# Indexer keys gathered once and transposed on TensorE, indexer queries projected before the keys

## The chip, the core and the metric

The kernel runs on one core of one Trainium2 chip. The metric is the device time of one execution in microseconds (us), the median of three runs. A kernel is one program with an instruction stream for each engine: TensorE (PE in the profile; its weight loads are PEld), VectorE (DVE), ScalarE (ACT), GpSimd (POOL) and SyncE (SP). Each engine works through its stream in order and waits on semaphores for the others. SP, POOL and ACT also issue DMA transfers.

## The reference, cut to what matters

One step of a two-layer decoder trunk, for a prompt of 256 tokens and for 8 sample sequences of 4 tokens (288 columns together). Layer 0 has sparse attention: an indexer scores all earlier keys of each token, the best `k_sel` are chosen, and attention runs over those alone.

```python
def index_select(qi, wi, ki, q_pos, key_pos, k_sel):
    dots = jnp.einsum('thd,sd->ths', qi, ki, preferred_element_type=jnp.float32)
    score = jnp.einsum('th,ths->ts', wi.astype(jnp.float32) * IDX_W_SCALE, jax.nn.relu(dots))
    causal = key_pos[None, :] <= q_pos[:, None]
    _, idx = lax.top_k(jnp.where(causal, score, -jnp.inf), k_sel)
    ...
def attn_layer_sample(x, cache_k, cache_v, cache_ki, page_table, w_in, w_out):
    q, k, v, qi, ki, wi = project_attn(x, w_in)
    q, k, qi, ki = rope_all(q, k, qi, ki, pos_new)
    ki_past = cache_ki[page_table].reshape(Bd, PAST_LEN, IDX_DIM)
    ...
```

For the samples the indexer keys lie in a paged cache: 16 pages of 128 positions with 64 numbers each for every sequence, 128 pages or 4 MB in all, and 256 positions are chosen from 2,052. The prompt chooses 64 of its own at most 256. After attention come the output projection, a ConvFFN, a Conformer convolution layer and a second ConvFFN.

## The kernel before, in words

All projections are matmuls in split precision. `K.pump` (L136 to 166) loads a slab of raw weights (`raw`, 128x1024, 512 KB) from SP's queue, ScalarE rounds it to `wh` (L158), and VectorE subtracts to get `wl` (L160; for slabs marked `pool` GpSimd does it). TensorE then does three matmuls for each 128x128 block (L227 to L229, called a projection matmul below). `raw` has five buffers, `wh` and `wl` three.

Everything up to the queries is written as one projection after another, with other work let in between. `K.gemm` calls `tick` after each few matmuls, and `tick` pays credit to lanes of generators (`ev`, `norms`, `bg`, `bg2`); a generator issues some instructions and yields a price. This happens while the program is built, so what results is a fixed order on each engine.

The order before: `x` is loaded and split into `xh` and `xl`; `g_idx[0]` gives the indexer keys and head weights (`kiw`); `g_k` the attention keys; `g_idx[1]` and `g_idx[2]` the indexer queries `qi` (rotated on VectorE by `rope`, L687 to L691); `g_q` the queries in four groups; then `k.drain` issues all that is left in the lanes, and `g_v` follows (L1083). Beside it run:

- The indexer keys of the samples. Four indirect DMAs from GpSimd's queue gather a quarter of every page each (1 MB), each is written to a buffer `kid` in DRAM (L667), and `load_kx` (L669) reads it back from ScalarE's queue (L672) with the 64 dimensions on partitions: two sequences to a tile `kx[pr]`.
- `prompt_index(half)`: dots of the prompt's queries with its keys for 8 of the 16 heads (L1000), Relu (L1003), weighted sums on VectorE (`pacc`, L1014). Half 0 is put in behind `g_idx[1]`, half 1 into the sample's dots; after half 1 eight rounds of MAX and MATCH_REPLACE for each of two token tiles find the 64 best (L1026, L1027), at price `TOPK`.
- `sample_index` (L800): copies `qi` into a block matrix `qiblk` (L806), 16 dot matmuls over the keys (L831), Relu (L834), weighted sums over heads on TensorE (`wsum`, L824) into four strips of 32 rows; then a bisection in 31 steps for the threshold (VectorE counts at L879, TensorE adds over partitions at L861), a compaction in 9 rounds and 8 shifts to a list of 256 indices (L936 to L964), a transpose (L970), and the indirect gathers of keys and values (`kv_load`, L654).
- `prepare` (L774): constants for the selection, on GpSimd and VectorE.

## Time and profile before

| | |
|---|---|
| median of 3 runs | 2657.99 us (2655.25 to 2664.32) |
| the profiled execution | 2659.64 us |
| its span, first to last instruction | 2657.9 us |
| TensorE busy | 2554.7 us, 96% |
| VectorE, ScalarE, GpSimd busy | 61%, 44%, 23% |
| weights read by SP's queue (q1) | 396.46 MB |

What lies outside the span is 1.7 us. Times in the rows below count from the start of the span. [...] A chain is read as start, length, what; a list of instructions has start, length, engine, line and operands, and in brackets how long the engine had been idle and what released it.

### The profile page before, as it was taken

Reading aid. Unit: us, or ns where it says so; the run is one execution under the profiler, and the core shown is the slowest. Engines: PE = TensorE matmul, PEld = TensorE weight load, DVE = VectorE, ACT = ScalarE, POOL = GpSimd, SP = SyncE. Lnnn points to the kernel's source line nnn. Section 1 sums busy time; section 2 is a strip of 40 time slices with the busy share of each in tenths; the row PEclk is TensorE's granted clock in tenths of the full one; section 3 lists DMA queues with packets and bytes.
Section 4 is the critical chain, followed back from the end, with each engine's and each line's share of the span. In section 5 each row is a group of like instructions: output and inputs, shape, how many; then the busy total and the mean of one; then the engine's idle time right before and its main releaser. Section 6 shows DMA issues by size and latency. Waiting matters only on the chain.

```text
span 2657.9 us, 49546 instructions
## 1 busy us (share of the span) xinstructions
PE 2554.7 (96%) x19608; PEld 2457.8 (92%) x19608; DVE 1623.3 (61%) x2546; ACT 1161.7 (44%) x1801; POOL 619.1 (23%) x857
## 2 busy tenths in 40 slices
PE   8799799999999999999998999899999999999997
PEld 7678766999999999999998898899999999999997
DVE  4458654677665445555658888778555444555554
ACT  4344343455444334444446444656444333444334
POOL 2130342252222101011136444343101000101123
PEclk9899899999999999999999999999999999999999
DMA  9724765556555455554644677454555445555643
GB/s 337 183 80 127 246 242 195 180 158 202 172 159 168 166 167 159 169 164 159 173 162 136 164 181 190 159 170 151 167 169 165 162 161 171 159 172 162 171 161 107
DMA packets 410552, 454.90 MB, mean 171 GB/s; under 512 B 34816, under 2 KB 338608, under 8 KB 409168
## 3 DMA queue, kind: packets, MB, share of 16 engines
q1 hardware_dynamic: 389600, 396.46, 48.3%
q0 software_dynamic: 12400, 51.09, 5.7%
q10 hardware_dynamic: 8320, 4.19, 0.8%
q8 instruction: 153, 2.51, 0.4%
q14 instruction: 79, 0.65, 0.1%
HBM read 438.37 MB, written 13.30 MB: 170 GB/s over the span
## 4 chain that ended last, share of the span: by engine, by line
PE 85%; DVE 5%; DMA 4%; POOL 2%; issue 2%; ACT 1%; SPq 0%; ACTq 0%; DVEq 0%; POOLq 0%
PE pt L229 25%; PE pt L228 25%; PE pt L227 25%; DVE wl L160 2%; PE pg L227 1%; DMA kvt<-kiT,pgq 1%; PE pg L228 1%; PE pg L229 1%; PE pt L1638 1%; PE tr L1178 1%; ACT wh L158 1%; DMA kvt<-kvc,idxS 1%; PE pg L831 1%; PE pg L1000 1%; DMA xt<-spread 1%
## 5 line engine op out<-in xcount | busy, mean ns | idle before, releaser
L160 DVE TENSOR_TENSOR wl<-raw,wh 128x1024 fp32r<-128x1024 f32 (+2 forms) x709 | 884.4, 1251 | 783.3 <-ACT wh L158 771.3
L158 ACT ACTIVATE wh<-raw 128x1024 fp32r<-128x1024 f32 (+1 forms) x726 | 760.2, 1051 | 940.3 <-PE pt L228 686.2
L229 PE MATMUL pt<-xh,wl 128*128 128x288 f32 (+1 forms) x3520 | 1039.9, 295 | 6.2 <-DVE wl L160 6.1
L227 PE MATMUL pt<-xh,wh 128*128 128x288 f32 (+1 forms) x3520 | 1042.1, 296 | 0.8 <-ACT xh L1297 0.8
L228 PE MATMUL pt<-xl,wh 128*128 128x288 f32 (+1 forms) x3520 | 1042.1, 296 | 0.1
L229 PEld LDWEIGHTS pt<-xh,wl 128*128 128x128 f32 x3520 | 665.6, 189 | 7.8 <-DVE wl L160 7.8
L227 PEld LDWEIGHTS pt<-xh,wh 128*128 128x128 f32 x3520 | 662.9, 188 | 7.8 <-issue 4.9
L228 PEld LDWEIGHTS pt<-xl,wh 128*128 128x128 f32 x3520 | 663.4, 188 | 0.5 <-DVE xl L1298 0.3
L229 PE MATMUL pt<-hh,wl 128*128 128x288 f32 (+1 forms) x1664 | 495.6, 298 | 2.9 <-DVE wl L160 2.9
L227 PE MATMUL pt<-hh,wh 128*128 128x288 f32 (+1 forms) x1664 | 493.3, 296 | 1.2 <-ACT wh L158 1.2
L228 PE MATMUL pt<-hl,wh 128*128 128x288 f32 (+1 forms) x1664 | 493.8, 297 | 0.0
L229 PEld LDWEIGHTS pt<-hh,wl 128*128 128x128 f32 x1664 | 312.9, 188 | 3.8 <-DVE wl L160 3.8
L227 PEld LDWEIGHTS pt<-hh,wh 128*128 128x128 f32 x1664 | 313.4, 188 | 2.3 <-ACT wh L158 2.1
L228 PEld LDWEIGHTS pt<-hl,wh 128*128 128x128 f32 x1664 | 313.9, 189 | 0.2
L1413 POOL COPY sto<-gpad 128x2 f32<-128x2 f32 x88 | 82.0, 932 | 963.5 <-ACT gpad L1406 963.3
L227 PE MATMUL pg<-xh,wh 128*128 128x288 f32 (+1 forms) x464 | 143.5, 309 | 10.0 <-ACT wh L158 9.3
L229 PE MATMUL pg<-xh,wl 128*128 128x288 f32 (+1 forms) x464 | 140.2, 302 | 3.5 <-DVE wl L160 3.4
L228 PE MATMUL pg<-xl,wh 128*128 128x288 f32 (+1 forms) x464 | 139.9, 301 | 0.1
L1417 ACT ACTIVATE s<-y,pvec 128x304 f32<-128x304 f32 x88 | 48.4, 550 | 161.6 <-DVE y L1412 161.6
L227 PEld LDWEIGHTS pg<-xh,wh 128*128 128x128 f32 (+1 forms) x464 | 89.2, 192 | 13.1 <-ACT wh L158 9.9
L302 POOL TENSOR_TENSOR lns<-lns,x 128x288 f32<-128x288 f32 x56 | 53.0, 946 | 185.3 <-DVE x L1326 177.8
L229 PEld LDWEIGHTS pg<-xh,wl 128*128 128x128 f32 (+1 forms) x464 | 89.2, 192 | 5.4 <-DVE wl L160 5.4
(389 smaller groups left out, 2419.3 us busy)
## 6 DMA issues: line engine op xcount, KB each, us to landing
raw<-w_ffn_gate SPq DMA_DIRECT2D x352, 256.0 KB, 2.9
raw<-w_ffn_up SPq DMA_DIRECT2D x352, 256.0 KB, 3.2
raw<-w_ffn_down SPq DMA_DIRECT2D x169, 512.0 KB, 3.6
raw<-w_attn_in SPq DMA_DIRECT2D x64, 512.0 KB, 4.5
raw<-w_pw SPq DMA_DIRECT2D x128, 256.0 KB, 4.5
raw<-w_attn_out SPq DMA_DIRECT2D x32, 512.0 KB, 4.7
raw<-w_pw SPq DMA_DIRECT2D x32, 512.0 KB, 4.3
xt<-spread SPq DMA_DIRECT2D x60, 136.0 KB, 2.9
```

The costliest lines, as they stand in the source:

```text
L158: nc.scalar.activation(wh[:, :n], r[:, :n], AF.Copy)
L160: eng.tensor_tensor(wl[:, :n], r[:, :n], wh[:, :n].bitcast(F32), op=OP.subtract)
L227: nc.tensor.matmul(out, wh[:, c:c + w], xh, start=st, stop=False)
L228: nc.tensor.matmul(out, wh[:, c:c + w], xl, start=False, stop=False)
L229: nc.tensor.matmul(out, wl[:, c:c + w], xh, start=False, stop=sp)
L302: nc.gpsimd.tensor_tensor(self.s1, self.s1, self.x[:, j], op=OP.add)
L831: nc.tensor.matmul(p[:, :512], qb[:, pr], kx[pr][:, 512 * i:512 * i + 512], start=True, stop=True)
L1000: nc.tensor.matmul(p[:, i * nk:(i + 1) * nk], qi[q_:q_ + 64, h // 2, tt * 128:(tt + 1) * 128], ki[q_:q_ + 64, :nk], start=True, stop=True)
L1178: nc.tensor.transpose(p[:, h * 128:(h + 1) * 128], g[:, h * 128:(h + 1) * 128], ident)
L1413: nc.gpsimd.tensor_copy(sto[:, j, 0:2], gp[:, 256:258])
L1417: nc.scalar.activation(s[:, :304], y[:, :304], AF.Silu, bias=k.par(bc, j))
L1638: nc.tensor.matmul(p[32 * i:32 * i + 32, :TP], dg[:, i, m - PEM], xt[:, i, 4 * (m - PEM):4 * (m - PEM) + TP], start=m == PEM, stop=m == 7, ...
```

## The change

The pages are gathered once, by four indirect DMAs of 1 MB, from a cache laid out as rows of 32 positions times 64 dimensions. Two of them fill a new tile `pages`; the other two fill the buffer named `x`, which held the input until it was split. There is no `kid` and no read back. 16 times four TensorE transposes turn 128x128 pieces, whose columns lie 32 numbers apart, into PSUM, and ScalarE and VectorE take turns to copy each bank of 512 columns into place in `kvA` (`load_kx`, priced by `KXW`). The indices for the gathers are computed on GpSimd. The keys now have the two halves of a sequence's pages on the two halves of the partitions, so the dots go by sequence (8 times 2 matmuls) and the weighted sums by two strips of 64 rows. The indexer queries come ahead of `g_k`, whose slabs are now split on GpSimd too. Prompt half 0 goes into the sample's dots; half 1 and the prompt's rounds go in behind them on lane `bg2`, at `TOPK` 5.0.

```diff
--- before.py
+++ after.py
-TOPK = 2.6
+TOPK = 5.0
...
-KXD = (42.0, 4.2)
+KXW = (11.0, 2.6)
...
     g_idx = [k.add(Group([(win, KIC, 80)], [80], NT, 8))]
+    g_idx += [k.add(Group([(win, QIC + 512 * i, 512)], [128] * 4, NT, 2)) for i in range(2)]
     g_k = k.add(Group([(win, KC, 512)], [128] * 4, NT, 2))
-    g_idx += [k.add(Group([(win, QIC + 512 * i, 512)], [128] * 4, NT, 2)) for i in range(2)]
     g_q = [k.add(Group([(win, QC + 512 * i, 512)], [128] * 4, NT, 2)) for i in range(4)]
     g_v = [k.add(Group([(win, VC + 256 * i, 256)], [128] * 2, NT, 4)) for i in range(2)]
-    for g in g_q[:2]:
+    for g in [g_k] + g_q[:2]:
         for s_ in g.slabs:
             s_.pool = True
...
-    pgi = bp.tile([128, 1], I32, name="pgi")
+    pgi = bp.tile([128, 2], I32, name="pgi")
+
+    for u in range(2):
+        for g in range(2):
+            nc.gpsimd.dma_start(pgi[64 * u:64 * u + 64, g:g + 1],
+                                bass.AP(tensor=pt.tensor, offset=pt.offset + 8 * g, ap=[[NPG, NS], [1, 8], [1, 1]]))
     nc.gpsimd.dma_start(tab, bass.AP(tensor=pt.tensor, offset=pt.offset, ap=[[0, 128], [1, 128]]))
-    nc.gpsimd.dma_start(pgi, bass.AP(tensor=pt.tensor, offset=pt.offset, ap=[[1, 128], [1, 1]]))
...
+    pgq = bp.tile([128, 2, 2], I32, name="pgq")
+    for u in range(2):
+        for i in range(2):
+            nc.gpsimd.tensor_scalar(pgq[64 * u:64 * u + 64, i], pgi[64 * u:64 * u + 64], 4.0, float(2 * u + i),
+                                    op0=OP.mult, op1=OP.add)
...
-    kid = tc.dram_tile([NS * NPG, ID * PAGE], F32, name="kid")
-    kx = [kvA.tile([128, 2, 1024], F32, name="kvt").rearrange("p a b -> p (a b)") for _ in range(4)]
-    pgq = bp.tile([128, 4], I32, name="pgq")
-    for i in range(4):
-        nc.vector.tensor_scalar(pgq[:, i:i + 1], pgi, 4.0, float(i), op0=OP.mult, op1=OP.add)
-    kq = a["kiT"].rearrange("(a d) c -> a (d c)", d=ID // 4)
-
-    for i in range(4):
-        gather(kx[i], kq, pgq[:, i:i + 1])
-        nc.gpsimd.dma_start(kid[:, 2048 * i:2048 * i + 2048], kx[i])
+    kvA = ap.tile([128, 4, 2, 1024], F32, name="kvA")
+    kx = kvA.rearrange("p r a b -> p (r a b)")
+    pgs_ = [gp0.tile([128, 4096], F32, name="pages"), base.tile([128, NT, T], F32, name="x")]
+    pgs_[1] = pgs_[1].rearrange("p j t -> p (j t)")[:, :4096]
+    for i in range(2):
+        for g in range(2):
+            gather(pgs_[i][:, 2048 * g:2048 * g + 2048], a["kin"], pgq[:, i, g:g + 1])
 
     def load_kx():
-        yield KXD[0]
-        for b in range(NS):
-            nc.scalar.dma_start(kx[b // 2][64 * (b % 2):64 * (b % 2) + 64].rearrange("d (g c) -> d g c", c=PAGE),
-                                kid[b * NPG:(b + 1) * NPG].rearrange("g (d c) -> d g c", c=PAGE))
-            yield KXD[1]
-
-    k.bg.append(load_kx())
+        nonlocal sp
+        yield KXW[0]
+        to = kx.rearrange("p (g u s) -> p u g s", u=2, s=64)
+        for n in range(16):
+            src = pgs_[n // 8].rearrange("p (gd s) -> p s gd", s=PAGE // 4)
+            p = pb()
+            for i in range(4):
+                nc.tensor.transpose(p[:, 128 * i:128 * i + 128], src[:, 4 * (n % 8) + i], ident)
+            frm = p[:, :512].rearrange("p (s u g) -> p u g s", s=4, u=2)
+            if n % 2:
+                nc.vector.tensor_copy(to[:, :, :, 4 * n:4 * n + 4], frm)
+            else:
+                nc.scalar.activation(to[:, :, :, 4 * n:4 * n + 4], frm, AF.Copy)
+            yield KXW[1]
+        stG.close()
+        sp = stB.enter_context(tc.tile_pool(name="sel", bufs=1))
+
+    k.bg2.append(load_kx())
...
-        for s in range(2):
+
+        for g in range(2):
             for par in range(2):
-                src = qi[par * 64:(par + 1) * 64, :, TP:].rearrange("p j (r s t) -> p r s j t", s=2, t=TS)[:, :, s]
-                dst = qb[s * 64:(s + 1) * 64].rearrange("p r (s j e t) -> p r s j e t", s=2, e=2, t=TS)[:, :, s, :, par]
+                src = qi[par * 64:(par + 1) * 64, :, TP:].rearrange("p j (b t) -> p b j t", t=TS)
+                dst = qb[g * 64:(g + 1) * 64, :, g * 64:(g + 1) * 64] \
+                    .rearrange("p b (j e t) -> p b j e t", e=2, t=TS)[:, :, :, par]
                 nc.vector.tensor_copy(dst, src)
...
         k.drain(k.ev)
-        others = prompt_index(1)
+        S, zer, code, powi, iot = (se[n] for n in ("S", "zer", "code", "powi", "iot"))
+        others = prompt_index(0)
...
-            for i, pr, rl in u:
-                nc.tensor.matmul(sc[32 * i:32 * i + 32, :512], ws[:, pr], rl, start=(pr == 0), stop=(pr == 3),
+            for c, b, rl in u:
+                nc.tensor.matmul(sc[64 * c:64 * c + 64, :512], ws[:, b], rl, start=(b == 0), stop=(b == NS - 1),
                                  skip_group_check=True)
...
-        for pr in range(4):
+        for b in range(NS):
             done, todo = todo, []
-            for i in range(4):
+            for c in range(2):
                 p = pb()
-                nc.tensor.matmul(p[:, :512], qb[:, pr], kx[pr][:, 512 * i:512 * i + 512], start=True, stop=True)
-                rl = bp.tile([128, 512], F32, name="rls", bufs=3) if i else \
-                    bp.tile([128, 512], F32, name="rlx", tag="xst", bufs=2)
+                nc.tensor.matmul(p[:, :512], qb[:, b], kx[:, 1024 * b + 512 * c:1024 * b + 512 * c + 512],
+                                 start=True, stop=True)
+                rl = bp.tile([128, 512], F32, name="rls", bufs=3)
                 nc.scalar.activation(rl, p[:, :512], AF.Relu)
-                todo.append((i, pr, rl))
-                if i == 0:
-                    wsum(done)
-                elif i % 2 and pr + i < 6:
-                    next(others)
+                todo.append((c, b, rl))
+            wsum(done)
+            if b < 6:
+                next(others)
...
         dots_done.append(1)
+        k.bg2.append(rest_of_prompt(others))
...
-        yield from others
+
+    def rest_of_prompt(first):
+        yield from first
+        yield from prompt_index(1)
...
-        if half == 0:
-            while k.ev.q:
-                yield 0.4
-            p = pb()
-            for tt in range(2):
-                nc.tensor.transpose(p[:, 16 * tt:16 * tt + 16], kiw[64:80, tt * 128:(tt + 1) * 128],
-                                    ident[64:80, 64:80])
-            nc.vector.tensor_scalar(wt, p[:, :32], IDX_W, None, op0=OP.mult)
-            yield 0.4
...
+    def prompt_weights():
+        yield 6.0
+        p = pb()
+        for tt in range(2):
+            nc.tensor.transpose(p[:, 16 * tt:16 * tt + 16], kiw[64:80, tt * 128:(tt + 1) * 128], ident[64:80, 64:80])
+        nc.vector.tensor_scalar(wt, p[:, :32], IDX_W, None, op0=OP.mult)
+        yield 0.4
+
+    k.bg.append(prompt_weights())
...
-    ps = k.gemm(g_k, xin, pg)
-    evac_rope(0, ps, [kT[:, m] for m in range(4)],
-              lambda: nc.sync.dma_start(o["k"].rearrange("(j p) t -> p j t", p=128), kT))
-
     for gi in range(2):
         ps = k.gemm(g_idx[gi + 1], xin, pg)
         for m in range(4):
             nc.scalar.activation(qi[:, 4 * gi + m], ps[m][:, :T], AF.Copy)
         k.ev.append(rope_qi(gi))
-        if gi == 0:
-            k.bg2.append(prompt_index(0))
 
     k.bg.append(sample_index())
 
 
+    ps = k.gemm(g_k, xin, pg)
+    evac_rope(0, ps, [kT[:, m] for m in range(4)],
+              lambda: nc.sync.dma_start(o["k"].rearrange("(j p) t -> p j t", p=128), kT))
...
-    a["kiT"] = c(g["cache_kidx"][0].transpose(0, 2, 1)).reshape(POOL * ID, PAGE)
+    a["kin"] = c(g["cache_kidx"][0].reshape(POOL, 4, PAGE // 4, ID).transpose(0, 1, 3, 2)).reshape(POOL * 4, -1)
```

On GpSimd the first queue entries of the program change. Before:

```order
L630 DMA tab<-page_table 128x128
L631 DMA pgi<-page_table 128x1
L639 DMA ident<-ident 128x128
L640 MEMSET ones_d 128x128
L641 MEMSET ones_h 128x128
L642 MEMSET eps 128x1
L654 DMA kvt<-kiT,pgq 128x2048
L667 DMA kid<-kvt 128x2048
L654 DMA kvt<-kiT,pgq 128x2048
```

In the changed kernel:

```order
L637 DMA pgi<-page_table 64x1x1 x4
L639 DMA tab<-page_table 128x128
L647 DMA ident<-ident 128x128
L648 MEMSET ones_d 128x128
L649 MEMSET ones_h 128x128
L650 MEMSET eps 128x1
L654 ISA
L654 TENSOR_SCALAR pgq<-pgi 64x2 x4
L667 DMA pages<-kin,pgq 128x2048 x2
L667 DMA x<-kin,pgq 128x2048 x2
```

Before, the first gather waits for `pgq`, which VectorE computes behind all of its splits of `x`; now `pgq` is GpSimd's own, and two gathers stand in its queue behind nothing but small entries.

On TensorE the end of the indexer's projections and the start of the sample's dots read as follows before (`kvt` holds the keys):

```order
L229 MATMUL pg<-xh,wl 128x288
L831 MATMUL pg<-kvt,qiblk 128x512 x2
L1000 MATMUL pg<-ki,qi 128x128 x4
L831 MATMUL pg<-kvt,qiblk 128x512 x2
L1000 MATMUL pg<-ki,qi 128x128 x4
L831 MATMUL pg<-kvt,qiblk 128x512
L824 MATMUL pg<-rlx,wsel 32x512
L824 MATMUL pg<-rls,wsel 32x512 x3
```

And in the changed kernel:

```order
L232 MATMUL pg<-xh,wl 128x288
L841 MATMUL pg<-kiw,con 128x32
L866 MATMUL pg<-kvA,qiblk 128x512 x2
L1030 MATMUL pg<-ki,qi 128x128 x4
L866 MATMUL pg<-kvA,qiblk 128x512 x2
L859 MATMUL pg<-rls,wsel 64x512 x2
L1030 MATMUL pg<-ki,qi 128x128 x4
L866 MATMUL pg<-kvA,qiblk 128x512 x2
L859 MATMUL pg<-rls,wsel 64x512 x2
```

The dots stand three projection matmuls behind the indexer's queries in both; sums of four strips became twice as many sums of two.

On VectorE the compaction reads before as follows (`x_` and `m_` are the list and its mask):

```order
L160 TENSOR_TENSOR wl<-raw,wh 128x1024
L936 TENSOR_SCALAR m__2402<-x__2372 128x512
L938 SCALAR_TENSOR_TENSOR x__2404<-m__2402,x__2372 128x512
L939 COPY_PREDICATED x__2404<-m__2402,x__2372 128x504
L160 TENSOR_TENSOR wl<-raw,wh 128x1024
L936 TENSOR_SCALAR m__2431<-x__2404 128x512
```

And in the changed kernel:

```order
L163 TENSOR_TENSOR wl<-raw,wh 128x1024
L972 TENSOR_SCALAR m__2314<-x__2284 128x512
L974 SCALAR_TENSOR_TENSOR x__2316<-m__2314,x__2284 128x512
L975 COPY_PREDICATED x__2316<-m__2314,x__2284 128x480
L1056 MAX m_2319<-pacc_245 128x8
L1057 MATCH_REPLACE pacc_245<-m_2319,pacc_245 128x256
L163 TENSOR_TENSOR wl<-raw,wh 128x1024
L972 TENSOR_SCALAR m__2346<-x__2316 128x512
```

The prompt's rounds now stand inside the compaction. From the matmul of the second sum to the transpose of the list there are 11 `wl` and no round before, 8 `wl` and 6 rounds now. From `g_v` on the order is the same on every engine but for buffer names.

## Rows read from the trace of the kernel before

**Rows 1.** Busy time by stretch, from the first keys' projection to `g_v`.
```profile
18.80:77.10 58.30, 54.85 (x387) 53.21 (x387) 25.74 (x38) 22.98 (x35) 11.89 (x19) 0.97 0.98 345
126.10:157.50 31.40, 31.39 (x124) 14.45 (x124) 7.95 (x20) 13.32 (x23) 0.00 (x0) 0.92 0.00 1
233.20:273.80 40.60, 36.53 (x272) 36.01 (x272) 37.81 (x69) 15.92 (x23) 0.42 (x1) 1.00 0.47 140
283.60:321.60 38.00, 30.85 (x204) 29.77 (x204) 23.50 (x60) 11.78 (x16) 10.92 (x10) 0.87 0.67 240
```

**Rows 2.** TensorE's waits up to 450 us: total us, times, longest.
```profile
PE pg L227 <- ACT wh L158: 9.3, 2, 8.2
PE pg L1000 <- DVE wtok L989: 8.1, 1, 8.1
PE pg L831 <- issue: 6.9, 1, 6.9
PE sc L229 <- DVE wl L160: 6.3, 1, 6.3
PE pg L861 <- DVE yes L883: 4.5, 2, 3.6
PE pg L970 <- DVE lst L963: 3.6, 1, 3.6
PE pg L229 <- DVE wl L160: 3.4, 6, 0.7
```

**Rows 3.** The chain that ended last, up to 80 us.
```profile
6.15 8.91 DMA x<-xT
...
60.24 8.33 DMA kid<-kvt
68.63 0.65 ACTq L672
```

**Rows 4.** Busy time by stretch, while `x` is loaded.
```profile
10.00:15.20 5.20, 4.43 (x27) 3.87 (x26) 3.82 (x10) 3.63 (x10) 0.00 (x0) 1.00 1.09 359
```

**Rows 5.** DMA queues from 22 to 25 us: packets, MB, share of 16 engines.
```profile
q0 software_dynamic: 125, 0.98, 78.2%
q1 hardware_dynamic: 126, 0.24, 20.4%
```

**Rows 6.** Busy time by stretch, where the clock was granted at half.
```profile
72.90:76.30 3.40, 3.40 (x16) 3.40 (x15) 1.09 (x1) 1.02 (x3) 0.00 (x0) 0.50 1.21 217
79.80:90.00 10.20, 4.79 (x25) 4.07 (x25) 7.10 (x14) 1.71 (x3) 0.00 (x0) 0.50 0.62 132
223.10:226.50 3.40, 3.40 (x16) 3.40 (x17) 2.94 (x7) 1.36 (x2) 0.41 (x1) 0.50 0.02 5
294.80:301.60 6.80, 3.28 (x13) 3.28 (x14) 5.59 (x11) 0.00 (x0) 3.15 (x2) 0.50 0.32 88
```

**Rows 7.** Pieces of TensorE in the chain (an fp32 matmul leaves two records).
```profile
135.54 1.00 PE pg L824 x8
...
138.65 1.91 PE pg L831 x4
...
153.58 0.79 PE pg L842 x8
...
333.77 0.59 PE tr L1178 x4
```

**Rows 8.** VectorE's instructions in order of time.
```profile
125.09 0.92 DVE L806 COPY qiblk<-qi 64x128 f32<-64x128 f32 x4
...
179.53 0.16 DVE L888 TENSOR_SCALAR fl<-pg 128x1 int32<-128x1 f32 x1 [0.48 <-PE pg L861]
...
288.82 0.43 DVE L1026 MAX8 m<-pacc 128x8 f32<-128x256 f32 x1
...
289.36 0.41 DVE L1027 MATCH_REPLACE8 pacc<-m,pacc 128x256 f32<-128x256 f32 x1
```

**Rows 9.** Groups of instructions by form, 233.2 to 273.8 us.
```profile
L160 DVE TENSOR_TENSOR wl<-raw,wh 128x1024 fp32r<-128x1024 f32 x11 | 13.4, 1215 | 1.4 <-ACT wh L158 1.4
```

More of the change, by code (lines that the diff above doesn't have):

```diff
@@ L75 @@
 _o = 0
-for _n, _w in (("bones", 128), ("lower", 128), ("esel", 128), ("wmask", 4 * 32),
+for _n, _w in (("bones", 128), ("lower", 128), ("esel", 128), ("wmask", TS),
                ("cq", T), ("sq", T), ("tri", 128), ("ncaus", 4), ("blk", 32),
@@ L849, in sample_index @@
         p = pb()
-        for pr in range(4):
-            nc.tensor.matmul(p[96:128, :4], ws[:, pr], rn[:, 4 * pr:4 * pr + 4], start=(pr == 0), stop=(pr == 3))
-        nc.vector.tensor_tensor(S[96:128, 512:], p[96:128, :4], cc("ncaus", 96, 128), op=OP.add)
+        for b in range(NS):
+            nc.tensor.matmul(p[96:128, :TS], ws[:, b, 32:], rn[:, TS * b:TS * b + TS], start=(b == 0),
+                             stop=(b == NS - 1))
+        nc.vector.tensor_tensor(S[96:128, 512:], p[96:128, :TS], cc("ncaus", 96, 128), op=OP.add)
         dots_done.append(1)
+        k.bg2.append(rest_of_prompt(others))
         scr = sp.tile([128, W1], I16, name="scr", bufs=2)
@@ L1747, in _consts @@
     put("bones", same.astype(f))
-    put("lower", (same & (p[:, None] // 32 < p[None, :] // 32)).astype(f))
+    quarter = np.repeat(np.array(QUARTERS), 32)
+    put("lower", (same & (quarter[:, None] < quarter[None, :])).astype(f))
     hrow = (p % 64) // TS
     put("esel", (np.arange(NI)[:, None] == hrow[None, :]).astype(f), 64)
-    tok = (2 * np.arange(4)[None, :, None] + (p // 64)[:, None, None]) * TS + (p % TS)[:, None, None]
-    put("wmask", ((tok == np.arange(32)[None, None, :]) * IDX_W).astype(f).reshape(128, 128))
+    put("wmask", ((p % TS)[:, None] == np.arange(TS)[None]).astype(f) * f(IDX_W))
     pos = np.concatenate([np.arange(TP), np.tile(PAST + np.arange(TS), NS)]).astype(f)
```

59 lines of the change are left out of this document (36 added, 23 removed).

## Prediction

> **What bounds the kernel now.** The page's head comes first: TensorE is busy 96% of the span, so only three kinds of thing in the part that changes can move the end: a TensorE wait that comes or goes, TensorE work that comes or goes, and stretches at half clock while TensorE works. The stretches of the first 322 us come next: in [rows 1] TensorE is busy 54.9 of 58.3 us beside the first projections, 31.4 of 31.4 in the sample's dots, 36.5 of 40.6 in the compaction, 30.9 of 38.0 in `g_v`. Third are TensorE's waits [rows 2]: 8.1 us for the prompt's weights `wtok`, 6.9 before the first sample dot (put down to nothing, but VectorE ends its copies to `qiblk` at 126.0 us [rows 8], and the dot starts at 126.1), 6.3 for `wl` in `g_v`, 4.5 in the bisection, 3.6 for the list. The chain of work [rows 3] shows where the round trip is felt: the load of `x`, later the last write of `kid` (8.3 us), and ScalarE's read at 68.6 us, behind which its rounding `wh` stands. The reader is to see that the trip itself is nearly hidden; what shows is what was queued behind it.
>
> **The start.** Before, the page gathers waited for VectorE's last split of `x`. Now two stand near the head of GpSimd's queue, while `x` is still coming in: the chain ends that load at 15.1 us [rows 3], the DMA engines are full there (share 1.09, 359 GB/s) [rows 4]. When a page gather and SP's loads meet, the gather takes 78% of the engines' time and SP 20% [rows 5]. The two bring 2.1 MB, 5.8 us of a full DMA at 359 GB/s. If they begin before `x` is in, it comes up to 5.8 us later; if behind it, 0. I take +4.5, nearer the upper end, because their indices need only a small load issued first of all. The longer wait also risks a stretch at half clock: one of 3.4 us, as behind the 3.6 us wait at 223 us [rows 6], costs 1.7; I take +0.9. **+5.4 (0 to 7.5).**
>
> [...]
>
> **The first projections.** ScalarE's wait for `kid` is gone, with the waits behind it: 1.1 us for `wh` (9.3 less the 8.2 at the start) and two of 0.7 for `wl` [rows 2], and the 3.4 us at half clock that follow [rows 6], 1.7. **-4.2 (0 to -5).** The same 387 projection matmuls stand here; which columns they make does not matter. Added are 16 groups of four transposes. A group of the same shape takes 0.59 us in attention [rows 7], and refilling the projections behind it a little: 0.63, **+10.1 (9.4 to 20, see the rivals).** The copies out of PSUM lie on ScalarE and VectorE, 23.0 and 25.7 us busy of 58.3 [rows 1], and cost nothing while that holds; were they bare, 16 of about 0.7 us would stand there.
>
> **Prompt half 0.** Behind `g_idx[1]` its dots waited 8.1 us for `wtok` and the rotation on VectorE. It moves into the sample's dots, long after that, and the wait goes: **-8.1.** The 10.2 us at half clock around it hold 4.8 us of TensorE work [rows 6], worth up to 2.4; I take **-1.5**, since the same small matmuls come back one by one elsewhere. Half 1 leaves the dots and comes into `g_k`: the same TensorE work, no change.
>
> **The wait before the dots** stays. The dots still stand three matmuls behind the last indexer query, and behind them on VectorE come rotation and copies. Queued behind the waiting dot is all of TensorE. The four copies take 0.92 us [rows 8] and are twice as wide now: **+0.5 (0.2 to 0.9).**
>
> **The dots.** 16 of 128x512 as before: two in 1.91 us [rows 7]. Four sums side by side took 1.00 us; now two side by side go eight times instead of four: 8.0 for 4.0 us, +4.0, if two strips of 64 overlap as four of 32 did (bound: 1.91 a pair, +11). The dots with the new keys are 8 instead of 4, 0.79 us more [rows 7]. **+4.8.**
>
> **The bisection** runs 204 projection matmuls earlier, over `g_k` and the first queries, whose `wl` GpSimd makes. Of its two waits of 4.5 us, 0.9 is a rotation of queries on VectorE and 3.6 a rotation plus a `wl` [rows 2]; now two rotations without `wl` stand in it, 1.8. The half clock behind the longer one (3.4 us [rows 6]) goes, 1.7. Nine rounds of the prompt come in. VectorE idles 0.48 us in each step [rows 8], a round takes 0.95 over 256 columns, and eight of the nine go over 128; I take 1.2 in all (0 to 6). **-3.2.**
>
> **The compaction** is where VectorE limits: 37.8 of 40.6 us busy [rows 1], and TensorE waits 3.6 for its list. Six rounds of 0.95 come in, three `wl` of 1.215 [rows 9] go out, +2.1 on VectorE, which end at the same 270 matmuls: the wait grows to 5.7, with up to 1.7 of half clock, 0.9 taken. **+3.0 (0 to 4).** What is late behind it is the first gathers of keys and values, but 249 matmuls follow instead of 42, so attention does not see it.
>
> **`g_v`.** Before, all rounds left over stood on VectorE ahead of its `wl`: 6.3 us, and half of 3.3 us of TensorE work at half clock [rows 6]: **-7.9.** From there on the order is unchanged.
>
> **The sum:** +5.4 -4.2 +10.1 -8.1 -1.5 +0.5 +4.8 -3.2 +3.0 -7.9 = -1.1 us against the profiled execution's 2659.64 us (span 2657.9 and 1.7 around it), which is 1.65 above the median: 2658.5 there, **2657.0** against the runs' median of 2657.99. What can be told from no change is about 0.3%, 8 us.
>
> **Rival 1, faster: the added work finds room.** The small index load takes so long in a full DMA that the gathers start behind `x` (start 0, not +5.4), and VectorE's 2.8 idle us in the compaction take up the rounds (0, not +3.0). Then -9.5: 2648.5. For it: the first gather can't start before its index has landed among full queues. Against: 78 to 20 [rows 5] needs only a small overlap.
>
> **Rival 2, slower: the transposes are dear.** They load a stationary piece whose columns lie 32 numbers apart; no row shows that, the 0.59 is for columns in a row. If a group takes twice as long, 1.26 us, 16 cost 20.2: +9.0 in all, 2667.1. From about 1.2 us a group it decides. [...]
>
> **Rival 3, the start costs more.** The second pair of gathers, issued as soon as `x` is split, takes 6 us of 78% again while the first `raw` slabs are due; three `wl` late by 1 to 2 us make +4: 2661. Against: before, four gathers and four writes of `kid` met the same slabs and TensorE was still busy 54.9 of 58.3 us.
>
> **Chances and range.** Forecast 0.43, rival 1 0.31, rival 2 0.13, rival 3 0.11, rest 0.02. Faster by over 0.3% is most of rival 1 and the forecast's lower tail, 0.33; slower is rival 2 and an upper tail, 0.17; 0.50 between. The range goes from rival 1 less some microseconds to rival 2: 2643 to 2668. The forecast's own is 2651 to 2663.
>
> **What would show it.** The load of `x` ends at 19 to 20 us; no wait for `wtok` and none of 6 us in `g_v`; groups of transposes of 0.6 us, 1.2 under rival 2; 6 to 8 us before the first dot; pairs of sums in 1.0 us; over 5 us before the list's transpose. The forecast is wrong if `x` comes no later, if a wait of over 4 us appears at the first transposes (pages not there), or if attention, whose order is the same, changes by over 3 us.

## The result, and the profile after

The changed kernel took 2684.32 us, the median of five runs (2675.48 to 2685.3), against 2661.34 of the kernel before (five runs, 2655.25 to 2664.32): a ratio of 1.0082, interval 1.006 to 1.0103. It is slower by about 0.8%, and outside the range forecast. The profiled execution took 2685.3 us, its span 2683.5; the mean granted clock was 0.978 against 0.986.

The busy time by stretch comes first. Its columns, as in [rows 1], [rows 4] and [rows 6], are the stretch, its length, the busy time of PE, PEld, DVE, ACT and POOL with the number of instructions, the granted clock as a share of full speed, the busy share of the DMA engines, and GB/s. Its first row is everything up to attention, and the line under the view is the same stretch before.

```profile
0.00:348.05 348.05, 307.63 (x1901) 274.51 (x1901) 203.65 (x487) 126.41 (x195) 91.79 (x78) 0.89 0.48 152
25.30:32.20 6.90, 6.73 (x28) 6.40 (x28) 0.11 (x1) 0.03 (x1) 0.00 (x0) 0.51 1.02 400
39.00:88.30 49.30, 49.30 (x379) 49.05 (x377) 27.29 (x33) 21.02 (x29) 5.64 (x5) 1.00 0.53 156
90.20:107.30 17.10, 8.85 (x16) 4.12 (x16) 9.78 (x19) 2.39 (x4) 3.53 (x4) 0.50 0.12 34
107.30:134.60 27.30, 27.30 (x105) 11.40 (x105) 4.30 (x11) 10.95 (x19) 0.00 (x0) 1.00 0.00 1
134.60:161.90 27.30, 27.30 (x101) 22.35 (x100) 14.21 (x47) 5.58 (x8) 2.36 (x1) 0.50 0.07 19
232.30:280.20 47.90, 41.37 (x274) 40.38 (x274) 45.72 (x84) 15.89 (x23) 8.78 (x4) 0.89 0.41 120
318.05:348.05 30.00, 29.14 (x205) 28.29 (x205) 11.72 (x14) 11.79 (x16) 7.81 (x8) 0.94 0.58 206
```

```profile
0.00:321.60 321.60, 273.76 (x1820) 248.39 (x1820) 192.90 (x491) 121.49 (x187) 71.75 (x65) 0.94 0.61 191
```

Attention starts 26.4 us later and carries 25.6 to the end. Those 26.4 us can be split by what TensorE did. Idle time is the stretch less its busy time. The cost of half clock is an estimate, half of the busy time in the stretches where the clock was granted at half. The first matmuls are counted in, up to 11.5 us before and 15.1 after: the profile has no clock for them, but they follow each other every 0.24 us, as later ones do at half clock, and not every 0.133. What remains is work. Before: 47.8 us idle, 14.9 half clock, 258.9 work. After: 40.4, 36.8 and 270.8. So the change took 7.4 us of waits away and added 11.9 of work; the forecast's terms, added up in the same way, took 11.3 of waits away and added 14.9 of work. But the change also added 21.9 us of half clock, where the forecast took 4.75 off: that is nearly the whole miss. The stretch to see is 134.6 to 161.9: TensorE busy for all of 27.3 us, at clock 0.50.

TensorE's waits up to 450 us (total us, times, longest), beside [rows 2]:

```profile
PE pg L230 <- ACT wh L161: 11.2, 4, 5.8
PE pg L866 <- DVE qiblk L838: 10.1, 1, 10.1
PE pg L897 <- DVE cnt L960: 3.6, 1, 3.6
PE pg L1006 <- DVE lst L999: 3.4, 1, 3.4
PE pg L897 <- DVE gt L931: 3.2, 1, 3.2
PE pg L232 <- DVE wl L163: 2.8, 5, 0.7
```

The waits for `wtok` (8.1) and in `g_v` (6.3) are gone; the one before the sample's dots grew from 6.9 to 10.1.

**Start.** ScalarE in order of time, then the DMA queues from 16 to 28 us, as in [rows 5]:

```profile
15.21 1.45 ACT L255 ACTIVATE xh<-x 128x288 fp32r<-128x288 f32 x4 [0.20 <-DMA x<-xT]
...
16.86 1.06 ACT L161 ACTIVATE wh<-raw 128x1024 fp32r<-128x1024 f32 x1 [0.21 <-DMA raw<-w_attn_in]
23.10 1.06 ACT L161 ACTIVATE wh<-raw 128x1024 fp32r<-128x1024 f32 x1 [5.18 <-DMA raw<-w_attn_in]
...
32.17 1.06 ACT L161 ACTIVATE wh<-raw 128x1024 fp32r<-128x1024 f32 x1 [7.72 <-DMA raw<-w_attn_in]
```

```profile
q0 software_dynamic: 493, 3.65, 73.1%
q1 hardware_dynamic: 492, 1.33, 28.3%
```

`x` is in at 15.2 us, against 15.06 before [rows 3]. GpSimd had its last index computed at 10.7 us and issued the first gather at 11.06, but the gathers' queue (q0) moved no packet from 12 to 15 us. What comes late are the two slabs behind `x`: the four gathers run back to back and hold 73% of the DMA engines.

**The wait before the dots.** VectorE and then GpSimd, in order of time:

```profile
85.44 3.31 DVE L817 CAST tb<-tab 32x32 f32<-32x32 int32 x4
...
92.09 2.72 DVE L709 TENSOR_TENSOR rsh<-rsh,coni 128x1024 f32<-128x1024 f32 x1
94.73 1.21 DVE L711 TENSOR_TENSOR qi<-qi,coni 128x1024 f32<-128x1024 f32 x1
...
97.12 1.19 DVE L838 COPY qiblk<-qi 64x256 f32<-64x256 f32 x4
```

```profile
84.99 2.41 POOL L163 TENSOR_TENSOR wl<-raw,wh 128x1024 fp32r<-128x1024 f32 x1 [1.24 <-ACT wh L161]
...
91.39 2.34 POOL L163 TENSOR_TENSOR wl<-raw,wh 128x1024 fp32r<-128x1024 f32 x1
```

`prepare` waits for the buffer of the pages, so its casts now stand right ahead of the last rotation, and they took 3.31 us beside GpSimd (0.73 before the change, at 26.5 us). The multiplication at 92.09 took 2.72 us, its twin at 94.73, with GpSimd through at 93.73 (91.39 and 2.34), 1.21. In the kernel before it stood beside a `wl` of GpSimd too, for a shorter time, and took 2.03. Those two lines of the kernel before:

```profile
119.32 2.38 POOL L160 TENSOR_TENSOR wl<-raw,wh 128x1024 fp32r<-128x1024 f32 x1 [1.24 <-ACT wh L158]
...
120.75 2.03 DVE L688 TENSOR_TENSOR rsh<-rsh,coni 128x1024 f32<-128x1024 f32 x1
```

So the multiplication took 1.51 us more than its twin with 1.64 us of GpSimd's `wl` beside it (93.73 - 92.09), and 0.82 us more with 0.95 beside it (121.70 - 120.75) before. That it stands still for nearly as long as GpSimd still works is my estimate from these times; the trace has one record for the whole of it.

**The end of the bisection.** VectorE and then GpSimd, in order of time:

```profile
216.55 2.64 DVE L733 TENSOR_TENSOR rsh<-rsh,con 128x288 f32<-128x288 f32 x1
...
228.66 3.36 DVE L958 TENSOR_TENSOR_SCAN scr<-gt,zer 128x512 int16<-128x512 int16 x1
```

```profile
216.50 2.37 POOL L163 TENSOR_TENSOR wl<-raw,wh 128x1024 fp32r<-128x1024 f32 x1 [2.97 <-PE pg L897]
...
228.60 2.34 POOL L163 TENSOR_TENSOR wl<-raw,wh 128x1024 fp32r<-128x1024 f32 x1 [1.54 <-ACT wh L161]
```

In the kernel before, where no `wl` of GpSimd stands there, these two took 0.46 and 1.22 us. TensorE's waits for `gt` (3.2 us) and `cnt` (3.6) lie behind them.

**The dots, and what follows them.** TensorE in order of time:

```profile
125.61 1.98 PE L866 MATMUL pg<-kvA,qiblk 128*128 128x512 f32 x4
127.52 1.08 PE L859 MATMUL pg<-rls,wsel 128*64 128x512 f32 x4
128.53 1.98 PE L866 MATMUL pg<-kvA,qiblk 128*128 128x512 f32 x4
...
131.45 1.95 PE L876 MATMUL pg<-kn,qiblk 128*128 128x4 f32 x16
133.33 1.08 PE L859 MATMUL pg<-rls,wsel 128*64 128x512 f32 x4
134.34 0.88 PE L885 MATMUL pg<-rn,wsel 128*32 128x4 f32 x16
135.15 0.61 PE L230 MATMUL pg<-xh,wh 128*128 128x288 f32 x1
...
136.17 2.07 PE L1030 MATMUL pg<-ki,qi 64*128 64x128 f32 x8
...
154.57 2.07 PE L1030 MATMUL pg<-ki,qi 64*128 64x256 f32 x4
```

From start to start, a pair of dots takes 1.91 us as before [rows 7] and a pair of sums 1.01: two strips of 64 do overlap. In the trace the records of a pair of sums start in twos (two at 130.4 us, two at 130.9), those of a pair of dots one by one (128.5, 129.1, 129.5 and 129.9). The clock falls at 134.6, with no wait ahead of it, while TensorE is in the second of two groups of matmuls of 4 columns (L876, L885), and returns 5 us after the last dots of half 1 (L1030).

### The profile page after: what moved, and what is told of

Same layout as the page of the kernel before. It is cut to its first block, busy times and chain, and to the rows that moved or that the text cites. A ratio compares the mean times of both kernels' runs of the same rounds, so it can differ in the third digit from the quotient of the medians.

```text
span 2683.5 us, 49723 instructions
## 1 busy us (share of the span) xinstructions
PE 2593.5 (97%) x19688; PEld 2487.9 (93%) x19688; DVE 1635.5 (61%) x2542; ACT 1166.7 (43%) x1809; POOL 639.2 (24%) x870
## 4 chain that ended last, share of the span: by engine, by line
PE 83%; DVE 3%; POOL 2%; ACT 1%; issue 1%; DMA 1%; SPq 0%; ACTq 0%; DVEq 0%; POOLq 0%
PE pt L231 25%; PE pt L232 25%; PE pt L230 25%; DVE wl L163 1%; PE pt L1673 1%; PE tr L1213 1%; PE m L1277 1%; PE sc L1234 1%; POOL x L488 0%; ACT wh L161 0%; PE tr L1163 0%; PE pg L232 0%; PE pg L230 0%; PE pg L231 0%; PE q L1185 0%
## 5 line engine op out<-in xcount | busy, mean ns | idle before, releaser
L163 DVE TENSOR_TENSOR wl<-raw,wh 128x1024 fp32r<-128x1024 f32 (+2 forms) x701 | 875.4, 1251 | 784.7 <-ACT wh L161 772.9
L230 PE MATMUL pg<-xh,wh 128*128 128x288 f32 (+1 forms) x464 | 152.1, 328 | 12.2 <-ACT wh L161 11.2
L232 PE MATMUL pg<-xh,wl 128*128 128x288 f32 (+1 forms) x464 | 146.1, 315 | 2.9 <-DVE wl L163 2.8
L231 PE MATMUL pg<-xl,wh 128*128 128x288 f32 (+1 forms) x464 | 145.9, 314 | 0.0
L232 PEld LDWEIGHTS pg<-xh,wl 128*128 128x128 f32 (+1 forms) x464 | 94.8, 204 | 4.8 <-DVE wl L163 4.8
```

The lines of the kernel that those rows point to most:

```text
L163: eng.tensor_tensor(wl[:, :n], r[:, :n], wh[:, :n].bitcast(F32), op=OP.subtract)
L230: nc.tensor.matmul(out, wh[:, c:c + w], xh, start=st, stop=False)
L231: nc.tensor.matmul(out, wh[:, c:c + w], xl, start=False, stop=False)
L232: nc.tensor.matmul(out, wl[:, c:c + w], xh, start=False, stop=sp)
```

## The experiments

Chips differ: the same kernel before had medians from 2658 to 2676 us on those used here. So each ratio below stands against runs of the kernel before on the same chip, and the changed kernel itself was one of the runs: it has two ratios, 1.0082 and 1.0062, and what an edit won is given against both where they differ. The clock is the mean over each one's runs (4 to 10 of it, 15 to 28 of the kernel before on its chip). By estimate from the changed kernel's span of 2683.5 us, 0.001 of clock is 2.7 us of TensorE time, where TensorE is busy all of it.

| run | ratio to before (interval) | clock, its own / before |
|---|---|---|
| c0_after | 1.0062 (1.0045 to 1.0079) | 0.9812 / 0.9848 |
| e1_halves | 1.0009 (0.9995 to 1.0023) | 0.9865 / 0.9843 |
| e4_half1_late | 1.0046 (1.003 to 1.0063) | 0.9830 / 0.9843 |
| e7_block | 1.0051 (1.0035 to 1.0067) | 0.9840 / 0.9848 |
| e10_cover | 1.0045 (1.0031 to 1.0059) | 0.9862 / 0.9855 |
| x1_before_half1 | 1.0011 (0.9995 to 1.0027) | 0.9844 / 0.9845 |
| x2_small | 1.0023 (1.0012 to 1.0034) | 0.9851 / 0.9855 |
| e2_later | 1.0037 (1.0019 to 1.0055) | 0.9855 / 0.9843 |
| e6_prepare | 1.0022 (1.0011 to 1.0033) | 0.9869 / 0.9848 |
| e3_pages | 1.0051 (1.0022 to 1.0081) | 0.9816 / 0.9843 |
| e5_spread | 1.0077 (1.0054 to 1.0099) | 0.9803 / 0.9848 |
| e8_gathers | 1.0008 (0.9993 to 1.0023) | 0.9834 / 0.9845 |
| e9_rounds | 1.0021 (1.001 to 1.0032) | 0.9841 / 0.9845 |
| b1_all | 0.9959 (0.9944 to 0.9974) | 0.9887 / 0.9845 |
| b2_copies | 0.9975 (0.9964 to 0.9985) | 0.9876 / 0.9855 |

### The half clock behind the dots

**Both halves among the dots (e1_halves).**

```diff
-        others = prompt_index(0)
+        others = prompt_both()
...
-            if b < 6:
+            if b < 7:
+                next(others)
                 next(others)
```

> Both halves of the prompt's dots stand among the sample's dots, as half 1 did before; nothing of half 1 is left behind them. In the changed kernel (profiled span 2683.5 us) TensorE works 27.3 us at half clock from 134.6 us on, with no wait ahead of it. Theory A: this comes from work that fills little of TensorE, the small matmuls that end the dots and then half 1's dots over 64 rows between the first projections. Without half 1 there the stretch is gone or 3.4 us long: 12 to 14 us less, some 2671 us. Rival B: the small matmuls alone bring it, whatever follows: a stretch of 7 us or more still begins at about 140 us, and at most 9 us are won. Rival C: it belongs to no piece of the program: no change beyond 3 us.

The stretch by time behind the dots, as in the first view:

```profile
133.00:160.00 27.00, 26.94 (x205) 26.69 (x205) 20.96 (x101) 7.83 (x8) 14.75 (x7) 1.00 0.36 101
```

Full clock, 205 matmuls where the changed kernel got 101 through, and 14 to 19 us won. (`prompt_both` yields from half 0 and then half 1.) Theory A and rival B differ in the place where a stretch would be, and there is none. Since one profile may lack the stretch by chance (see c0_after), the clock over ten runs counts for more: against the kernel before on its own chip it is 0.0058 higher than that of c0_after, 15 us.

**Half 1 later (e4_half1_late).** `rest_of_prompt` begins with `yield 25.0`.

> Half 1's dots come some 160 projection matmuls (22 us) later into the bisection, nothing else moves. Theory A (small matmuls and half 1 together): no long half clock behind the dots, and half 1 passes at full clock or with one stretch of 3.4 us: 10 to 13 us less, some 2672. Rival A2: half 1's dots among projections lower the clock by themselves: the stretch of over 20 us moves 22 us back with them, and the time stays within 3 us of 2683. Rival B: a stretch stays where the small matmuls end, and at most 9 us are won.

Stretches between the dots and half 1, and during half 1 (163.7 to 182.8 us):

```profile
142.00:162.00 20.00, 20.00 (x156) 20.00 (x155) 14.19 (x65) 8.14 (x14) 11.96 (x5) 1.00 0.47 134
...
165.70:186.20 20.50, 20.50 (x66) 15.95 (x65) 11.47 (x38) 6.56 (x11) 3.76 (x2) 0.50 0.33 106
```

The half clock moved back with half 1, as rival A2 said, but the time did not stay: 4 to 10 us better than the changed kernel, between A2's 3 and A's 10. A wait of 1.0 us stood just ahead of half 1 here.

**The changed kernel again (c0_after), and half 1 in one piece (e7_block).**

```diff
-        yield from prompt_index(1)
+        half1 = prompt_index(1)
+        for _ in range(7):
+            next(half1)
+        yield 7 * PRI
+        yield from half1
```

> The changed kernel itself, on the same chip as the three runs below, so that they have it for a measure. If the loss is the kernel's and not one chip's: 1.006 to 1.010 times the kernel before.

> The prompt's half 1 stands where the change put it, behind the sample's dots, but in one piece: its 16 dots follow each other, with no projections between them. Theory A2 (half 1's dots of 64 rows lower the clock when they alternate with projections; moved 22 us back, they took the half clock along): in one piece, 8 us of work, the clock falls for one or two short stretches or not at all, and 9 to 13 us are won on the changed kernel. Rival A3 (it is their amount, not how they are mixed): 16 in a row lower the clock at least as much, and the time stays within 4 us of the changed kernel's.

The profiled execution of c0_after has full clock where the first one had none:

```profile
132.30:159.60 27.30, 26.67 (x178) 23.78 (x178) 22.61 (x86) 8.77 (x11) 9.52 (x4) 1.00 0.21 59
```

So the long stretch belongs to some executions of the program and not to others; the mean clock over its runs is what can be compared. Attention starts at 338.9 us in this profile, not at 348.05.

In one piece half 1 did to the clock what A2 said: one stretch of 6.8 us at half behind it (143.8 to 150.6 us), and the mean rose from 0.9812 to 0.9840, worth 7.6 us. But only 3 us were won on the run beside it, which the intervals don't tell from nothing. Up to attention the profile of e7_block has 49.0 us of idle time, among it a wait of 6.4 us in the bisection; that of c0_after has 44.0. So neither A2's time nor A3's clock came out.

**Projections between the small matmuls (e10_cover).**

```diff
-        yield 0.7
+        yield 4.0
         wsum(todo)
...
     def rest_of_prompt(first):
+        yield 1.8
```

> In the changed kernel the small matmuls that end the sample's dots follow each other with nothing between (two matmul groups of 4 columns, 1.9 and 0.8 us, around the last sums); here 21 and 6 projection matmuls stand between them, and half 1 alternates with projections behind them as before. Theory A4 (these small matmuls drop the clock in part of the executions, and half 1, alternating, keeps it down until it is through; either alone does little): mean granted clock 0.984 to 0.987 instead of 0.980 to 0.981, 8 to 14 us less than the changed kernel, 1.001 to 1.004 times the kernel before. Rival A2 (half 1 alternating does it by itself): clock and time as in the changed kernel, 1.006 or more.

From the small matmuls to the end of half 1 at 146.4 us, and behind it:

```profile
125.00:152.00 27.00, 26.88 (x174) 21.13 (x175) 15.41 (x50) 8.64 (x13) 6.78 (x3) 1.00 0.14 40
152.00:165.00 13.00, 13.00 (x101) 13.00 (x101) 9.95 (x50) 4.40 (x5) 7.59 (x5) 1.00 0.45 125
```

The clock came back to that of the kernel before, 0.9862, with half 1 alternating as in the changed kernel. That is theory A4's clock; of its 8 to 14 us, 5 to 10 were won, and 1.0045 is just beyond what it gave. e4_half1_late won as much time at a lower clock, so it is the clock, not the time, that speaks for A4.

**The parts put into the kernel before (x1_before_half1, x2_small).** In the first, half 1 comes out of the dots and alternates with projections behind them; the second also drops the two yields between the small matmuls.

```diff
-                elif i % 2 and pr + i < 6:
-                    next(others)
...
         dots_done.append(1)
+        def half1():
+            yield 3.0
+            for _ in range(7):
+                yield next(others)
+        k.bg2.append(half1())
```

> The kernel before with one part of the change alone: half 1 of the prompt's dots is taken out of the sample's dots and put behind them, two to four dots at a time between projections, as in the changed kernel. The sum of the work is the same. Theory A (alternating with projections there, half 1 lowers the clock in part of the executions): slower than the kernel before by 6 to 16 us, with a mean granted clock 0.002 to 0.005 lower, and a stretch at half clock behind the dots. Rival C (the stretches of the changed kernel come from elsewhere): within 4 us of the kernel before, at its clock.

> The kernel before with half 1 alternating behind the dots, as in the last run on it, and also without the projections that stood between the small matmuls at the end of the dots (0.8 and 0.4 us there, half of the changed kernel's). Theory A4: the clock now falls behind the dots in part of the executions and stays down through half 1: mean clock 0.001 to 0.004 lower than the kernel before, 1.002 to 1.006. Rival C (the clock there is not set by these pieces): 1.000 to 1.002 again, at the clock of the kernel before.

Neither lowered the clock: half 1 passes at 1.00 in x1_before_half1,

```profile
148.50:161.00 12.50, 12.50 (x71) 9.72 (x71) 10.22 (x29) 4.33 (x7) 2.36 (x1) 1.00 0.15 42
```

and x2_small is slower by 0.23% at nearly the same clock, so not for theory A4's reason; what slowed it stays open. In the kernel before there are half as many small matmuls (4 and 4, not 8 and 8).

What follows: half 1 alternating behind the dots is not enough to lower the clock (1.00 in the views of x1 and e10), and it does not do so in each execution (1.00 in that of c0). In five profiles of kernels in which half 1 stands behind the dots and no projections were put between the small matmuls (the changed kernel, e3, e4, e5, e8) the clock fell between 1.6 us ahead of half 1's first dot and 2.9 us behind it, and in all five it returned 2 to 5 us after the last one, not before. Taking half 1 away (e1) or covering the small matmuls (e10) each brought the mean clock back (to 0.9865 and 0.9862). In e2 and e6 projections also came between the small matmuls, and their profiles too have no half clock there. That half 1 behind the dots costs 14 to 19 us of the changed kernel is shown by e1. I read the rest as two things that must meet: something lets the clock fall (the run of small matmuls, or a wait as the 1.0 us in e4, where the small matmuls were over 30 us past), and half 1 keeps it down. The profile of b2_copies, the last version below, shows the first without the second: half 1 is among the dots, no wait stands there, and the clock falls inside the second group of small matmuls (119.8 to 120.7 us) all the same, but returns after 6.8 us, with projections alone behind it:

```profile
120.10:126.90 6.80, 6.80 (x39) 6.78 (x37) 5.03 (x25) 0.62 (x1) 1.51 (x4) 0.50 0.00 1
```

In the five profiles with half 1 behind the dots it stayed down for 17 to 27 us. That the small matmuls let it fall rests on this, on e10, e2 and e6, and on the place where it fell in four of the five. It is not shown why they do so in one execution and not in another, and x2 did not show it in the kernel before.

### The wait before the dots

**Projections in its place (e2_later).** `yield 1.5` ahead of the dots becomes `yield 12.5`.

> The sample's dots come 75 projection matmuls (10.3 us) later in TensorE's order, so that these stand where it waited 10.1 us for VectorE's rotation and copies. Theory W: the wait goes, and with it the half clock behind it (17 us, half of 9.4 us of work): 12 to 15 us less, some 2670 us. Rival W2: the wait changes its place: the keys' projections need wl from GpSimd, which has the preparation of the selection in front of it; a wait of 5 us or more appears among them, and less than 6 us is won.

The wait was 5.9 us with the 75 projections in front of it, so it only shrank. VectorE ended its copies at 102.8 us instead of 98.3: beside four `wl` of GpSimd two steps of the rotation took 3.4 and 3.3 us (1.2 each in the changed kernel) and the copies 3.3. Theory W's 12 to 15 us were not reached, nor W2's 6 kept to: 7 to 12 were won, part of it perhaps because 12 of half 1's dots came in a row and projections between the small matmuls.

**Preparation behind the copies (e6_prepare).**

```diff
-        while sp is None:
+        while sp is None or not copied:
...
+        copied.append(1)
         yield 1.5
         while "S" not in se:
```

> The preparation of the selection stands behind the copies to qiblk, on VectorE and GpSimd, instead of ahead of the last rotation. Theory V: in the changed kernel the wait of 10.1 us before the sample's dots is VectorE beside GpSimd: four casts took 3.3 us (0.73 before), one multiplication of the rotation 2.7 instead of 1.2, while GpSimd ran. Without it the wait is 5.5 to 7.5 us. Rival V2: GpSimd's wl for the keys stand there in any case and slow the rotation as much: the wait stays at 9 us or more. Half 1's dots also come closer together here, which is worth up to 10 us by theory A2 above and is read apart, from the clock behind the dots.

VectorE, in order of time:

```profile
91.18 2.03 DVE L709 TENSOR_TENSOR rsh<-rsh,coni 128x1024 f32<-128x1024 f32 x1
93.13 1.41 DVE L711 TENSOR_TENSOR qi<-qi,coni 128x1024 f32<-128x1024 f32 x1
...
95.81 1.50 DVE L838 COPY qiblk<-qi 64x256 f32<-64x256 f32 x4
```

The wait fell to 7.8 us, a little over theory V's 5.5 to 7.5: two steps of the rotation still took 2.03 and 1.41 us (1.2 alone), which I put down to GpSimd's `wl`. 11 us were won on the run beside it. The clock rose to 0.9869, worth 15: here projections also came between the small matmuls, and half of half 1 in one piece.

### The start

**The second pair of gathers later (e3_pages), all four one by one (e5_spread), and the transposes later too (e8_gathers).** In the last, VectorE computes each index just before its gather:

```diff
-    for i in range(2):
-        for g in range(2):
-            gather(pgs_[i][:, 2048 * g:2048 * g + 2048], a["kin"], pgq[:, i, g:g + 1])
...
     def load_kx():
-        yield KXW[0]
+        for i, y in enumerate((3.0, 2.0, 6.0, 6.0)):
+            yield y
+            page(i // 2, i % 2)
+        yield KXW[0] - 17.0
...
-KXW = (11.0, 2.6)
+KXW = (22.0, 1.8)
```

> The second pair of page gathers is issued from within the transposes (at the second and the fourth group) instead of right behind the first pair. Theory S: in the changed kernel four gathers back to back (14.5 to 30 us) keep the first weight slabs of the indexer queries from coming: their rounding waits 5.2 and 7.7 us, TensorE waits 3.3 us and works at half clock for 10 us. With one pair there the second of these waits and the half clock behind it go: 6 to 9 us less, some 2676. Rival S2: the two later gathers starve other slabs in the same way: less than 3 us is won.

> The four page gathers come one by one, each held back by its index, which VectorE computes at four places between the weights of the first indexer queries; the transposes begin 33 projection matmuls later and stand closer together. Theory S3 (after the second pair alone, moved, won only 2 to 3 us): it is the first pair, right behind the load of x, that starves the first slabs. In the changed kernel the 120th projection matmul starts at 39.5 us against 28.1 in the kernel before; here it starts at 29 to 32, and 6 to 9 us are won up to the dots. Rival S4: the slabs are late for other reasons (they wait behind x and the constants on their own queue): the 120th starts at 36 us or later.

> The gathers one by one as in the last run on them, and the transposes begin another 57 projection matmuls later and stand 15 apart. Theory S3 (four gathers at once starve the first slabs; held back, they were only too late for the transposes, 6.4 us): the 120th projection matmul starts at 29 to 31 us, no wait for pages is left, and the sample's dots begin at 89 to 92 us instead of 98.0. Half 1 also comes closer together here, read apart. Rival S5: the slabs that the later gathers meet are late instead, and the dots begin at 95 us or later.

The 120th projection matmul started at 35.9, 29.2 and 29.6 us (28.1 in the kernel before, 39.5 in the changed one, 39.0 in c0_after). With the second pair alone later, the dots began at 94.9 us, 3 us before those of c0_after, and 3 to 8 us were won in all; S gave 6 to 9 and S2 less than 3, so that run settles neither. With all four one by one, the start is as S3 said, so it is the four together that make the slabs late. But e5_spread won nothing, and its transposes waited for the pages:

```profile
PE pg L691 <- DMA pages<-kin,pgq: 6.4, 1, 6.4
```

In e8_gathers no such wait is left, and the dots begin at 89.1 us instead of 98.0 (c0_after), as S3 gave; 14 to 20 us were won in all, 9 of them up to the dots.

### The compaction, and versions that beat both

**Rounds ahead of the compaction (e9_rounds).** On e1_halves, `TOPK` 2.6.

> As the first run (both halves among the sample's dots), and the prompt's rounds come closer (price 2.6 instead of 5.0), so that nearly all stand in the bisection and none in the compaction. Theory D: in the compaction (47 us from the second sum to the list, 41 before the change) the rounds are what makes VectorE late; without them it takes 40 to 43 us, and the bisection grows by less than 3 us: 3 to 6 us less than the first run's 1.0009. Rival D2: VectorE is as full in the bisection, which grows by what the compaction loses: within 3 us of the first run.

The compaction took 44.7 us, not 40 to 43, against 47 in the profile of e1_halves, and the bisection 81 us against 77. The whole was 3 us slower than e1_halves, which their intervals don't tell from no change. That is rival D2: the rounds cost in the bisection what they save here. In the compaction idle time fell to 3.9 us (6.5 in the changed kernel); half clock behind the wait at its start stayed (mean clock 0.90 from 217.3 to 262 us, 0.89 in the changed kernel's compaction).

**Three edits at once (b1_all), and the copies ahead of the prompt's rotation (b2_copies).** b1_all is e1_halves, e6_prepare and e8_gathers together; b2_copies has e1_halves and e8_gathers, `yield 4.0` between the two parts of the last rotation, the rest of `prepare` behind `dots_done`, and the prompt's dots from the third sequence on.

> Three edits at once on the changed kernel: both halves among the sample's dots, the preparation behind the copies to qiblk, the gathers one by one with the transposes later. If the three work apart from each other, 14 to 17 us for the first, 2 to 4 for the second (its other part was half 1 as well), 6 to 8 for the third: some 2665 us on this chip, 0.996 to 0.998 times the kernel before. If the start's gain is eaten by other slabs (rival S5) or by a longer wait before the dots: 1.000 or more.

> The best version so far (0.9959) with the wait before the dots taken down: the copies to qiblk stand ahead of the prompt's rotation, the preparation comes behind the dots, and the prompt's dots begin with the third sequence. Theory V (the wait of 7.9 us is rotation of the prompt's columns, 4.8 to 6.4 us of VectorE, and copies slowed by GpSimd): the wait is 2 to 4 us, the half clock behind it shorter, and 4 to 7 us are won: 0.993 to 0.9945. Rival V3: the prompt's dots or the bisection wait instead (over 3 us in one place), and less than 2 us is won.

TensorE's waits up to 310 us in b1_all:

```profile
PE pg L868 <- DVE qiblk L839: 7.9, 1, 7.9
PE pg L230 <- ACT wh L161: 7.0, 2, 5.7
...
PE pg L900 <- DVE cnt L963: 3.6, 1, 3.6
PE pg L1009 <- DVE lst L1002: 3.1, 1, 3.1
```

b1_all beats the kernel before by 0.41% and the changed one by 1.0 to 1.2%, just past what was expected of three edits that work apart. Its clock is 0.0042 above that of the kernel before, 11 us, which is all of its gain. In its profile, up to attention, idle time is 34.9 us (47.8 before) and work 268.8 (258.9): the waits that it saves pay for the work that the change adds, and little more. (The profiled run is the slowest of its six.) In b2_copies the wait fell to 4.7 us and idle time to 31.7, but attention began at the same time (317.6 and 317.3 us): half clock cost 19.9 us up to there, 13.6 in b1_all, in part behind the small matmuls and behind a wait of 5.0 us at the end of the bisection. That is rival V3.

## Why the prediction was wrong

**The step that failed is the clock.** The prediction put it as "Half 1 leaves the dots and comes into `g_k`: the same TensorE work, no change", and for half 0 took -1.5 "since the same small matmuls come back one by one elsewhere". The work was indeed the same, the clock behind it was not. But I priced half clock only behind waits, as 1.7 us here and there, in all -4.75; the profiled execution had +21.9, of which 13.7 is the one stretch behind the dots, with no wait ahead of it. Half 1 put back among the dots (e1_halves) won 14 to 19 us. Over the runs of c0_after the clock accounts for about 10 of its 18 us; the other 8 are work less the waits that went, for which the forecast had 3.6. What lets the clock fall is in part argued (see above).

- **Start, +5.4 forecast.** The 120th projection matmul is 11.4 us late, so the sign was right for a wrong reason. The 78 to 20 of [rows 5] was the right row, applied to the wrong transfer: `x` came no later, the sign that the prediction itself gave for being wrong, and the gathers' data came behind it, as in rival 1. Rival 3 named the slabs, at +4 and for the second pair; it was all four gathers, and half clock behind the waits.
- **Transposes, +10.1, and `kid`'s waits, -4.2.** From the 120th to the 432nd projection matmul it took 47.95 us before and 47.85 after, with 14 of the 16 groups in it: -0.1, where the two terms together are +5.9. From 39.0 to 88.3 us, 379 instructions hold 14 groups, and the 323 others at 0.133 us from start to start leave some 0.45 us for a group, 7 us in all. Rival 2 is wrong: columns 32 numbers apart cost nothing that shows from one transpose to the next, 110 ns against 109 in attention (L1213, columns in a row), though a weight load took 190 ns against 140. No run shows a group of 1.26 us, nor the 0.04 us that the forecast added to each for refilling.
- **`wtok` -8.1 and `g_v` -7.9.** Right: the first is gone, `g_v` takes 30.0 instead of 38.0 us.
- **The wait before the dots, +0.5.** Measured +3.2, and the half clock behind it lasted 17.1 us instead of 10.2 (from 120.7 us on in the kernel before). I costed the copies (+0.3 measured) and overlooked that `prepare` now waits for the transposes and lands ahead of the rotation, beside GpSimd's `wl` for `g_k`. The rest of the rotation began 1.6 us after its queries were there (89.68 us, not 88.05; none before), and its first multiplication took 0.7 us more.
- **The dots, +4.8.** Right: 32.0 us of work against 29.0, which held 1.6 of projections: +4.6.
- **The bisection, -3.2.** Idle time +2.6 instead, with waits of 3.2 and 3.6 us. I counted a rotation beside which GpSimd makes the `wl` as 0.9 us, its time alone; one step of it took 2.64 us beside a `wl` instead of 0.46, and a step of the count 3.36 instead of 1.22. c0_after has the same two, at 2.6 and 3.1.
- **The compaction, +3.0.** +7.0, 2.5 of idle time and 4.5 of half clock: the list waited 3.4 us, not 5.7, but a new wait of 2.8 us for `wh` came in (ScalarE's copies of the rotated queries stood behind VectorE's shifts, and `wh` behind them).

## What to carry to other kernels

Moving work of the same size is not free where TensorE is the bound: here, behind small matmuls in a row and with matmuls over 64 rows between full ones, it was busy at half clock for 27.3 us in one execution and at full clock in another, with no wait to show for it. So look at the granted clock of the stretch, and try full matmuls between the small ones (mean clock 0.9862 in e10_cover, 0.9855 in the kernel before on its chip). Compare such kernels by the mean clock over several runs, since one profile may or may not have the stretch. When gathers move to an earlier place, ask which transfer is due at the moment their data flows (here they held 73% of the DMA engines), and spread them; when VectorE's work lands beside GpSimd's, take its duration from a row where both run (2.64 us here, and 0.46 alone), also where GpSimd took the work off VectorE.

## What was not expected of the hardware

- Half clock without a wait: 27.3 us of TensorE busy throughout at clock 0.50 (134.6 to 161.9 us), present in one execution of the program and absent in another (c0_after, 1.00) at the same place.
- VectorE beside GpSimd: a multiplication or addition over 128x1024 took 1.2 us alone and up to 3.4 beside GpSimd's `wl`; a scan over 128x512 1.22 and 3.36; four casts of 32x32 0.73 and 3.31.
- Gathers that follow each other held 73% of the DMA engines for 12 us (3.65 MB) and left the weight queue 28% (1.33 MB); the slabs of 512 KB issued there took 14.4 us to land, against 3.6 for those from 40 to 88 us, when the gathers were through.
- Transposes with a stationary piece whose columns lie 32 numbers apart followed each other as fast as those of neighbouring columns: 110 ns from start to start, 109 in attention; a weight load took 190 ns against 140.
